# Attention with TensorE's products in source order, two heads' scores together, and low parts of weights by an adding DMA

## The chip, the core and the metric

The kernel runs on one core of one Trainium2 chip. The metric is the device time of one execution in microseconds (us). The engines of the core work beside each other, each in its own order: TensorE (PE in the rows; PEld is its weight load) multiplies into eight banks of PSUM, VectorE (DVE), ScalarE (ACT) and GpSimd (POOL) work on SBUF and PSUM, and SyncE (SP) issues the loads. An instruction waits, by semaphores, until what it reads is there and what it overwrites has been read.

## The reference, cut to what matters

Two layers on a sequence of 512 tokens with 1024 channels, batch 1, all in float32. Layer 0 mixes tokens by differential attention, layer 1 by retention; each layer goes on with a squared-ReLU MLP (1024 to 4096 and back) and a gated embedding. The change bears on the attention above all:

```python
qkv = xn @ w_qkv                                 # 8 heads; q and k: two halves of 64 each, v: 128
q = rms_norm(q, g_q) * (A_DHEAD ** -0.5)
k = rms_norm(k, g_k)
...
s = jnp.einsum('bqhcd,bkhcd->bhcqk', qb, k)      # c: the two halves
s = s + bias[None, :, None]                      # -slope of the head x distance
s = jnp.where(dist[None, None, None] >= 0, s, -jnp.inf)
a = jax.nn.softmax(s, axis=-1)
attn = a[:, :, 0] - lam * a[:, :, 1]
return jnp.einsum('bhqk,bkhe->bqhe', attn, v)
...
o = rms_norm(o, g_sub) * (1.0 - lambda_init)     # per head
return o.reshape(B, S, A_HEADS * A_VDIM) @ w_o
```

## The kernel before, in words

**Numbers in two parts.** Every matrix product is made of three: each float32 operand is split into a high part (`h`, rounded to float32r) and a low part (`l`, the rest), and `mm3` (L177) multiplies high by high, low by high and high by low into the same bank. In the rows the three have lines L179, L180 and L181.

**Weights.** `Weights.load` (L64) brings a block of 128x1024 float32 (512 KB) into one of three `raw` slots, ScalarE casts it to `wh` (L75), and `wl = raw - wh` is made by VectorE (L79). There are five slots each for wh and wl, so block i+5 can only be cast when the last product that reads block i is done. In the attention (blocks 8 to 35) the low part is shared: GpSimd makes one half of 512 columns, VectorE the other (L314).

**Attention.** Channels lie on partitions. The 8 heads go in four groups g of two. For each group and each tile tt of 128 tokens, `pqk` (24 products over the 1024 channels) gives q and k of the group's two heads; `norm_qk` (L346) takes their RMS over ScalarE and VectorE, `scale_qk` (L366) applies it, and `turn_qk` (L375) turns the tile by four transposes into the bank `ptqk`, from which ScalarE and VectorE write qh, ql, kh, kl. `scores(h, i)` (L395) makes the scores of head h for the i-th tile of queries: n = 128(i+1) columns of keys, two halves c of 64 rows, each with three products (kh by qh, kl by qh, kh by ql) into a bank `ps` of its own; the products of the two halves alternate in the source, since they use different rows of TensorE. VectorE evicts each half with the bias (L416), ScalarE exponentiates (L420), VectorE combines the two into `e`. `turn_a` (L433) turns e into `pt` and splits it into aT; `values` (L440) multiplies by v into the bank `po`; `sub_norm` (L453) sums the squares of po by two products into `pn`, ScalarE takes Ln, Exp and Square, VectorE L462 and L464 follow (L464 reads po), and `oT` goes into the output projection (`po__`, L501 on).

**Banks.** PSUM has three banks "mm" (pqk, pv, the projection), two "s" (scores), two "tr" (ptqk, pt, pn) and one "av" (po). A bank is taken again when its readers are done.

**What sets the order.** A plan (L469 to L547) gives each step a position in units of one three-product unit, and the steps are called in the order of these positions. The constants L_TURN, L_S, L_T, L_AV, L_N say how many units behind its inputs a step is called. This is the order of the source; a scheduler then orders each engine's instructions by its own estimate, and may move any product ahead of another. Only SP's loads are kept in program order.

**Layer 1.** Retention ends with eight up products `pu` (L794) whose banks ScalarE copies out (L797). The MLP (L556) begins with two tiles interleaved by `tiles` (L193); the column sums for its norm, `rsm1p`, are called at unit `late_at` of the second of them.

Of the kernel before, what the change touches and what calls it, by code (L numbers as in the profile page):

```python
# [12 lines left out]
AF = mybir.ActivationFunctionType  # L13
# [3 lines left out]
P = 128  # L17
T = 512
# [24 lines left out]
L_TURN = 6  # L43
L_S = 11
# [4 lines left out]
L_S2 = 0.5  # L49
# [3 lines left out]
class Weights:  # L53
# [3 lines left out]
    def __init__(self, tc, pool, order, ahead):  # L57
        self.tc, self.nc, self.pool, self.order, self.ahead = tc, tc.nc, pool, order, ahead
        self.made = []
        self.at = 0  # L60
        self.lo_engines = (self.nc.vector,)
        self.parts = 1

    def load(self):  # L64
# [5 lines left out]
        lo = self.pool.tile([P, 1024], F32R, name=f"wl{i}", tag="wl", bufs=W_BUFS)  # L70
        n = 1024 // self.parts
# [21 lines left out]
def decoder_trunk(ctx: ExitStack, tc, xT, pT, small, dist, decay, ident,  # L93
# [13 lines left out]
    def ps_s(name):  # L107
        return psum("s", 2, name)
# [67 lines left out]

    def mm3(ps, a, b, start, stop):  # L177

        nc.tensor.matmul(ps, a[0], b[0], start=start, stop=False)  # L179
        nc.tensor.matmul(ps, a[0], b[1], start=False, stop=False)  # L180
        nc.tensor.matmul(ps, a[1], b[0], start=False, stop=stop)  # L181
# [53 lines left out]
    def column_sums(ps, pair):  # L235

        nc.tensor.matmul(ps, ones_r, pair[0], start=True, stop=False)
        nc.tensor.matmul(ps, ones_r, pair[1], start=False, stop=True)
# [55 lines left out]
    with tc.tile_pool(name="at", bufs=1) as ap:  # L294
# [19 lines left out]
        W.lo_engines = (nc.gpsimd, nc.vector)  # L314
# [60 lines left out]
        def turn_qk(g, tt):  # L375
# [9 lines left out]
            for j in range(4):  # L385
                nc.tensor.transpose(pt[:, j * P : j * P + P], tf[:, j * P : j * P + P], idn)
# [8 lines left out]
        def scores(h, i):  # L395
            g, j = h // 2, h % 2
            q = (res[g, "q", "h"][:, j, :], res[g, "q", "l"][:, j, :])
            k = (res[g, "k", "h"][:, j, :], res[g, "k", "l"][:, j, :])
# [9 lines left out]
            pss = [ps_s(f"ps{h}{i}{c}") for c in range(2)]  # L408
            for m in range(3):
                for c in range(2):  # L410
                    rows = slice(DH * c, DH * c + DH)
                    a = q[1 if m == 2 else 0][rows, i * P : i * P + P]
                    b = k[1 if m == 1 else 0][rows, 0:n]
                    nc.tensor.matmul(pss[c][:, 0:n], a, b, start=m == 0, stop=m == 2)
            for c in range(2):
                nc.vector.tensor_tensor_reduce(  # L416
                    out=es[c], in0=pss[c][:, 0:n], in1=bias[h][:, T - n : T], op0=ALU.add, op1=ALU.min,
                    scale=1.0, scalar=3e38, accum_out=mn[h][:, i, c : c + 1],
                )
                nc.scalar.activation(  # L420
                    out=es[c], in_=es[c], func=AF.Exp, scale=-1.0, bias=mn[h][:, i, c : c + 1],
                    accum_out=su[h][:, i, c : c + 1],
                )
# [9 lines left out]
        def turn_a(h, kt):  # L433
            n = T - kt * P
            pt = ps_tr(f"pt{h}{kt}")
            for i in range(kt, NT):
                nc.tensor.transpose(pt[:, (i - kt) * P : (i - kt + 1) * P], eT[h, i][:, kt * P : kt * P + P], idn)
# [93 lines left out]
        for g in range(4):  # L531
            s = qk_at[g]
            for tt in range(NT):
# [3 lines left out]
                for j in range(2):  # L537
                    place(e + L_S + L_S2 * j, scores, 2 * g + j, tt)
            t0 = s + NT * KD - 1 + L_T[g]
            for j in range(2):  # L540
# [4 lines left out]
                place(tp + L_AV[g] + L_N, sub_norm, 2 * g + j)  # L545
        for _, _, fn, args in sorted(plan, key=lambda s: s[:2]):
            fn(*args)  # L547
        z, acc = zn, st["acc"]
        W.lo_engines = (nc.vector,)
# [6 lines left out]
    def mlp(z, acc, layer):  # L556
# [3 lines left out]
        with tc.tile_pool(name=f"mlp{layer}", bufs=1) as mp:  # L560
            for c in range(4):
# [14 lines left out]
                tiles(8, begin, unit, end, late if c == 0 else None)  # L576
# [67 lines left out]
    with tc.tile_pool(name="zp", bufs=1) as zp:  # L644
# [12 lines left out]
        with tc.tile_pool(name="ret", bufs=1) as ap:  # L657
# [135 lines left out]
            for m in range(KD):  # L793
                pu = ps_tr(f"pu1{m}")  # L794
# [7 lines left out]
        z, acc = mlp(z, acc, 1)  # L802
# [84 lines left out]
```

## Time and profile before

| | us |
|---|---|
| runs (three) | 1500.09, 1500.62, 1501.07; median 1500.62 |
| profiled execution | 1498.45 |
| its span, first to last instruction | 1496.6 |
| TensorE busy | 1470.9 (98%) |
| VectorE, ScalarE, GpSimd busy | 827.7, 618.7, 183.6 |
| chain that ended last: TensorE's share | 88% |
| attention in the trace | about 29 to 262 |

The chain is followed back from the last instruction, at each step to what released it. TensorE holds most of it, so a microsecond counts if TensorE stands or works longer than it need. Matmuls overlap in the pipeline, so the cost of a product is read as the step from its start to the next start, not as its own duration. "Idle before" in square brackets is time in which the engine had nothing to do before the instruction, with the instruction that released it.

### The profile page before, as it was taken

To read this page: it belongs to the slowest core of one execution; us is meant where nothing else is said; L and a number is where in the kernel's file an instruction comes from. 1 tells how busy PE (TensorE), PEld (TensorE's weight loads), DVE (VectorE), ACT (ScalarE), POOL (GpSimd) and SP (SyncE) were. 2 spreads that over 40 slices of the span, in tenths; PEclk is the share of its full clock that TensorE was granted. 3 is DMA by queue.
4 is the path that set the end of the run, shared out by engine and by line. 5 is a ranking of instruction groups with operands and counts; after the bars stand their busy time and mean duration, and the time that the engine had idled before them with its cause. 6 is when DMAs were issued, how large, how long until landed. Compare 5 with 4: busy or idle time off the path is not lost.

```text
span 1496.6 us, 17071 instructions
## 1 busy us (share of the span) xinstructions
PE 1470.9 (98%) x6668; PEld 1199.6 (80%) x6668; DVE 827.7 (55%) x1217; ACT 618.7 (41%) x966; POOL 183.6 (12%) x128
## 2 busy tenths in 40 slices
PE   9999999899999999999999999999999999999998
PEld 7667667688888888888888888888778888888887
DVE  7887888853434444475464564544584343434455
ACT  6666766541323224344442432433453241323332
POOL 4123223300000000311020110301220000000020
PEclk9999999999999999999999999999999999999999
DMA  6211131243333233232314233132233333333312
GB/s 234 61 57 57 57 113 57 81 116 99 98 92 95 96 99 99 85 99 93 105 51 132 64 99 106 57 127 71 71 99 99 98 94 93 96 98 99 99 57 85
DMA packets 40256, 137.90 MB, mean 92 GB/s; under 512 B 4464, under 2 KB 4976, under 8 KB 40176
## 3 DMA queue, kind: packets, MB, share of 16 engines
q1 hardware_dynamic: 40176, 136.82, 29.5%
q8 instruction: 52, 0.85, 0.2%
q14 instruction: 28, 0.23, 0.0%
HBM read 134.70 MB, written 2.10 MB: 91 GB/s over the span
## 4 chain that ended last, share of the span: by engine, by line
PE 88%; DVE 7%; ACT 2%; issue 1%; POOL 0%; DMA 0%; SPq 0%; POOLq 0%; DVEq 0%; ACTq 0%
PE py L179 8%; PE py L180 8%; PE py L181 8%; PE ph L180 8%; PE ph L181 8%; PE ph L179 8%; PE pg L181 2%; PE pg L180 2%; PE pg L179 2%; PE rv L180 2%; PE rqk L181 2%; PE rqk L180 2%; PE rv L181 2%; PE rv L179 2%; PE rqk L179 2%; PE rg L179 2%
## 5 line engine op out<-in xcount | busy, mean ns | idle before, releaser
L75 ACT CAST wh<-raw 128x1024 fp32r<-128x1024 f32 (+1 forms) x245 | 256.4, 1048 | 620.9 <-PE py L180 235.7
L79 DVE TENSOR_TENSOR wl<-raw,wh 128x1024 fp32r<-128x1024 f32 (+1 forms) x245 | 300.6, 1228 | 60.5 <-ACT wh L75 59.4
L180 PE MATMUL ph<-zl,wh 128*128 128x512 f32 x512 | 200.1, 391 | 3.5 <-DVE zl L160 3.4
L181 PE MATMUL ph<-zh,wl 128*128 128x512 f32 x512 | 199.8, 391 | 0.0
L179 PE MATMUL ph<-zh,wh 128*128 128x512 f32 x512 | 199.5, 390 | 0.1
L179 PE MATMUL py<-hh,wh 128*128 128x512 f32 x512 | 199.2, 389 | 0.0
L180 PE MATMUL py<-hl,wh 128*128 128x512 f32 x512 | 199.2, 389 | 0.0
L181 PE MATMUL py<-hh,wl 128*128 128x512 f32 x512 | 199.2, 389 | 0.0
L582 DVE TENSOR_TENSOR x<-x,py 128x512 f32<-128x512 f32 x64 | 44.0, 688 | 200.0 <-PE py L181 200.0
L572 DVE SCALAR_TENSOR_TENSOR ht<-ph,rsm 128x512 f32<-128x512 f32 x64 | 44.0, 691 | 158.8 <-PE ph L181 158.8
L180 PEld LDWEIGHTS ph<-zl,wh 128*128 128x128 f32 x512 | 96.5, 189 | 25.1 <-DVE zl L160 5.2
L179 PEld LDWEIGHTS ph<-zh,wh 128*128 128x128 f32 x512 | 96.4, 188 | 20.7 <-issue 0.5
L181 PEld LDWEIGHTS ph<-zh,wl 128*128 128x128 f32 x512 | 96.5, 189 | 20.1
L181 PEld LDWEIGHTS py<-hh,wl 128*128 128x128 f32 x512 | 96.1, 188 | 20.1
L179 PEld LDWEIGHTS py<-hh,wh 128*128 128x128 f32 x512 | 96.1, 188 | 20.0
L180 PEld LDWEIGHTS py<-hl,wh 128*128 128x128 f32 x512 | 96.1, 188 | 19.8
L229 POOL TENSOR_TENSOR acc_p<-acc_p,sq 128x512 f32<-128x512 f32 x14 | 24.2, 1727 | 673.7 <-ACT sq L228 673.7
L79 POOL TENSOR_TENSOR wl<-raw,wh 128x512 fp32r<-128x512 f32 x28 | 46.0, 1642 | 90.0 <-ACT wh L75 70.6
L179 PE MATMUL pqk<-wh,zh 128*128 128x512 f32 x128 | 53.6, 419 | 0.0
L179 PE MATMUL pg<-zh,wh 128*128 128x512 f32 (+1 forms) x136 | 51.2, 377 | 0.0
L181 PE MATMUL pg<-zh,wl 128*128 128x512 f32 (+1 forms) x136 | 51.2, 377 | 0.0
L180 PE MATMUL pg<-zl,wh 128*128 128x512 f32 (+1 forms) x136 | 51.2, 376 | 0.0
(874 smaller groups left out, 2762.9 us busy)
## 6 DMA issues: line engine op xcount, KB each, us to landing
raw<-in_w SPq DMA_DIRECT2D x128, 512.0 KB, 3.6
raw<-in_w_qk SPq DMA_DIRECT2D x16, 512.0 KB, 3.7
raw<-in_w_g SPq DMA_DIRECT2D x16, 512.0 KB, 3.6
raw<-in_w_rv SPq DMA_DIRECT2D x16, 512.0 KB, 3.7
raw<-in_w_rqk SPq DMA_DIRECT2D x16, 512.0 KB, 4.4
raw<-in_w_rg SPq DMA_DIRECT2D x16, 512.0 KB, 3.6
raw<-in_w_ro SPq DMA_DIRECT2D x16, 512.0 KB, 3.6
raw<-in_w_o SPq DMA_DIRECT2D x8, 512.0 KB, 3.6
```

Of the source, the lines that this page charges most:

```text
L75: nc.scalar.copy(out=hi[:, s], in_=raw[:, s])
L79: e.tensor_tensor(out=lo[:, r], in0=raw[:, r], in1=hi[:, r].bitcast(F32), op=ALU.subtract)
L179: nc.tensor.matmul(ps, a[0], b[0], start=start, stop=False)
L180: nc.tensor.matmul(ps, a[0], b[1], start=False, stop=False)
L181: nc.tensor.matmul(ps, a[1], b[0], start=False, stop=stop)
L229: nc.gpsimd.tensor_tensor(out=acc, in0=acc, in1=sq, op=ALU.add)
L572: nc.vector.scalar_tensor_tensor(out=t, in0=s[1], scalar=0.0, in1=rs, op0=ALU.max, op1=ALU.mult)
L582: nc.vector.tensor_tensor(out=x[m], in0=x[m], in1=ps, op=ALU.add)
```

## The change

Four edits. The products and transposes that the attention's plan calls are kept in the order of the source on TensorE (`pe`, `fixed`). `scores(g, i)` makes both heads of a group at once: for i = 0 and 1 (up to 256 columns) the heads share the two banks, each in its half of the columns, and their twelve products stand together; for i = 2 and 3 each head has its own two banks and its six products, one head after the other. L_TURN goes from 6 to 8 and L_S from 11 to 13 units. The low parts of blocks 8 to 35 are made by ScalarE, which writes -raw rounded into wl, and a DMA issued by GpSimd that adds raw to it; VectorE and GpSimd make no half of them any more. In layer 1 the up products alternate between the banks "tr" and "s", and the MLP's column sums are called at unit 5 in place of 2.

```diff
@@ -40,13 +40,12 @@
 RAW_BUFS, W_BUFS, SLOTS = 3, 5, 30
 
 L_SCALE = 4
-L_TURN = 6
-L_S = 11
+L_TURN = 8
+L_S = 13
...
-L_S2 = 0.5
...
@@ -68,6 +68,14 @@
         raw = self.pool.tile([P, 1024], F32, name=f"raw{i}", tag="raw", bufs=RAW_BUFS)
         hi = self.pool.tile([P, 1024], F32R, name=f"wh{i}", tag="wh", bufs=W_BUFS)
         lo = self.pool.tile([P, 1024], F32R, name=f"wl{i}", tag="wl", bufs=W_BUFS)
+        if self.by_dma:
+
+            self.tc.keep_in_program_order(nc.sync.dma_start(out=raw, in_=src))
+            nc.scalar.copy(out=hi, in_=raw)
+            nc.scalar.activation(out=lo, in_=raw, func=AF.Copy, scale=-1.0)
+            nc.gpsimd.dma_start(out=lo, in_=raw, accum_op=ALU.add)
+            self.made.append((hi, lo))
+            return
...
+    fixed = {"on": False}
+
+    def pe(ins):
+
+        if fixed["on"]:
+            tc.keep_in_program_order(ins)
+
     def mm3(ps, a, b, start, stop):
 
-        nc.tensor.matmul(ps, a[0], b[0], start=start, stop=False)
-        nc.tensor.matmul(ps, a[0], b[1], start=False, stop=False)
-        nc.tensor.matmul(ps, a[1], b[0], start=False, stop=stop)
+        pe(nc.tensor.matmul(ps, a[0], b[0], start=start, stop=False))
+        pe(nc.tensor.matmul(ps, a[0], b[1], start=False, stop=False))
+        pe(nc.tensor.matmul(ps, a[1], b[0], start=False, stop=stop))
...
@@ -311,7 +326,7 @@
             for tt in range(NT):
                 mm3(pv[tt], token(z[k], tt), block(w, k), k == 0, k == KD - 1)
         rst_columns(acc, rst, "prst0")
-        W.lo_engines = (nc.gpsimd, nc.vector)
+        W.by_dma = True
...
             tf = qkt.pop((g, tt))[0]
             pt = ps_tr(f"ptqk{g}{tt}")
             for j in range(4):
-                nc.tensor.transpose(pt[:, j * P : j * P + P], tf[:, j * P : j * P + P], idn)
+                pe(nc.tensor.transpose(pt[:, j * P : j * P + P], tf[:, j * P : j * P + P], idn))
...
-        def scores(h, i):
-            g, j = h // 2, h % 2
-            q = (res[g, "q", "h"][:, j, :], res[g, "q", "l"][:, j, :])
-            k = (res[g, "k", "h"][:, j, :], res[g, "k", "l"][:, j, :])
+        def scores(g, i):
+
+            n = P * (i + 1)
+            joint = n <= T // 2
+            pss = [ps_s(f"ps{g}{i}{c}") for c in range(2)] if joint else None
+            made = []
+            for j in range(2):
+                h = 2 * g + j
+                q = (res[g, "q", "h"][:, j, :], res[g, "q", "l"][:, j, :])
+                k = (res[g, "k", "h"][:, j, :], res[g, "k", "l"][:, j, :])
+                s = [pss[c][:, j * (T // 2) : j * (T // 2) + n] if joint else ps_s(f"ps{h}{i}{c}")[:, 0:n] for c in range(2)]
+                for m in range(3):
+                    for c in range(2):
+                        rows = slice(DH * c, DH * c + DH)
+                        a = q[1 if m == 2 else 0][rows, i * P : i * P + P]
+                        b = k[1 if m == 1 else 0][rows, 0:n]
+                        pe(nc.tensor.matmul(s[c], a, b, start=m == 0, stop=m == 2))
+                if joint:
+                    made.append((h, s))
+                else:
+                    weigh(h, i, s)
+            for h, s in made:
+                weigh(h, i, s)
+
+        def weigh(h, i, pss):
             if i == 0:
                 bias[h] = ap.tile([P, T], F32, name="bias", tag="bias", bufs=2)
                 nc.gpsimd.tensor_scalar(
@@ -405,16 +441,9 @@
                 su[h] = ap.tile([P, NT, 2], F32, name="su", tag="su", bufs=3)
...
-            pss = [ps_s(f"ps{h}{i}{c}") for c in range(2)]
-            for m in range(3):
-                for c in range(2):
-                    rows = slice(DH * c, DH * c + DH)
-                    a = q[1 if m == 2 else 0][rows, i * P : i * P + P]
-                    b = k[1 if m == 1 else 0][rows, 0:n]
-                    nc.tensor.matmul(pss[c][:, 0:n], a, b, start=m == 0, stop=m == 2)
             for c in range(2):
                 nc.vector.tensor_tensor_reduce(
-                    out=es[c], in0=pss[c][:, 0:n], in1=bias[h][:, T - n : T], op0=ALU.add, op1=ALU.min,
+                    out=es[c], in0=pss[c], in1=bias[h][:, T - n : T], op0=ALU.add, op1=ALU.min,
...
@@ -534,8 +563,7 @@
                 e = s + (7, 15, 30, 34)[tt]
                 place(e + L_SCALE, scale_qk, g, tt)
                 place(e + L_TURN, turn_qk, g, tt)
-                for j in range(2):
-                    place(e + L_S + L_S2 * j, scores, 2 * g + j, tt)
+                place(e + L_S, scores, g, tt)
...
@@ -543,17 +571,19 @@
                     place(tp, turn_a, 2 * g + j, kt)
                     place(tp + L_AV[g], values, 2 * g + j, kt)
                 place(tp + L_AV[g] + L_N, sub_norm, 2 * g + j)
+        fixed["on"] = True
         for _, _, fn, args in sorted(plan, key=lambda s: s[:2]):
             fn(*args)
+        fixed["on"] = False
         z, acc = zn, st["acc"]
-        W.lo_engines = (nc.vector,)
+        W.by_dma = False
...
-    def mlp(z, acc, layer):
+    def mlp(z, acc, layer, late_at=2):
...
-                tiles(8, begin, unit, end, late if c == 0 else None)
+                tiles(8, begin, unit, end, late if c == 0 else None, late_at)
...
             for m in range(KD):
-                pu = ps_tr(f"pu1{m}")
+                pu = (ps_tr if m % 2 == 0 else ps_s)(f"pu1{m}")
                 up_unit(pu, wu, p1, m)
                 t = zslot(f"pus{m}", F32)
                 nc.scalar.copy(out=t, in_=pu)
...
-        z, acc = mlp(z, acc, 1)
+        z, acc = mlp(z, acc, 1, late_at=5)
         gated_embedding(z, acc, None, 1, True, made=made)
```

Column sums and `turn_a` are wrapped in `pe` in the same way. Three places show what the order of the instructions becomes. In the names, the digits of `ps` are head (for i = 0 and 1 group), tile i and half c; those of `ptqk` and `pqk` are group and tile; those of `po`, `pn` are the head; `po05__` is the output projection.

TensorE, scores of the last tile (i = 3) of heads 0 and 1, before:

```order
L414 MATMUL ps030_800<-kh0_454,qh0_452 128x512
L414 MATMUL ps031_801<-kh0_454,qh0_452 128x512
L414 MATMUL ps030_800<-kl0_455,qh0_452 128x512
L414 MATMUL ps031_801<-kl0_455,qh0_452 128x512
L414 MATMUL ps030_800<-kh0_454,ql0_453 128x512
L414 MATMUL ps031_801<-kh0_454,ql0_453 128x512
L386 MATMUL ptqk10_819<-idn_314,qkt_721 128x128 x4
L179 MATMUL pqk11_735<-wh11_385,zh0_6_157 128x512
L414 MATMUL ps130_830<-kh0_454,qh0_452 128x512
L414 MATMUL ps130_830<-kl0_455,qh0_452 128x512
L414 MATMUL ps130_830<-kh0_454,ql0_453 128x512
L180 MATMUL pqk11_735<-wl11_386,zh0_6_157 128x512
```

and after:

```order
L426 MATMUL ps030_816<-kh0_476,qh0_474 128x512
L426 MATMUL ps031_817<-kh0_476,qh0_474 128x512
L426 MATMUL ps030_816<-kl0_477,qh0_474 128x512
L426 MATMUL ps031_817<-kl0_477,qh0_474 128x512
L426 MATMUL ps030_816<-kh0_476,ql0_475 128x512
L426 MATMUL ps031_817<-kh0_476,ql0_475 128x512
L426 MATMUL ps130_833<-kh0_476,qh0_474 128x512
L426 MATMUL ps131_834<-kh0_476,qh0_474 128x512
L426 MATMUL ps130_833<-kl0_477,qh0_474 128x512
L426 MATMUL ps131_834<-kl0_477,qh0_474 128x512
L426 MATMUL ps130_833<-kh0_476,ql0_475 128x512
L426 MATMUL ps131_834<-kh0_476,ql0_475 128x512
```

Before, head 1's halves stand apart, with products of pqk between; now all twelve stand in a row.

TensorE, the column sums of head 5 and the values of head 6, before:

```order
L237 MATMUL pn5_2549<-osq5h_2503,ones_r_67 128x512
L238 MATMUL pn5_2549<-osq5l_2504,ones_r_67 128x512
L180 MATMUL po06__2581<-oT0l_1177,wh27_1853 128x512
L181 MATMUL po06__2581<-oT0h_1176,wl27_1854 128x512
L179 MATMUL po06__2581<-oT1h_1384,wh27_1853 128x512
L180 MATMUL po06__2581<-oT1l_1385,wh27_1853 128x512
L181 MATMUL po06__2581<-oT1h_1384,wl27_1854 128x512
L179 MATMUL po06__2581<-oT2h_1557,wh27_1853 128x512
L180 MATMUL po06__2581<-oT2l_1558,wh27_1853 128x512
L181 MATMUL po06__2581<-oT2h_1557,wl27_1854 128x512
L179 MATMUL po06__2581<-oT3h_1731,wh27_1853 128x512
L180 MATMUL po06__2581<-oT3l_1732,wh27_1853 128x512
```

and after:

```order
L252 MATMUL pn5_2533<-osq5h_2487,ones_r_67 128x512
L253 MATMUL pn5_2533<-osq5l_2488,ones_r_67 128x512
L194 MATMUL po6_2548<-aT0h_2496,v101h_1153 128x512
L195 MATMUL po6_2548<-aT0l_2497,v101h_1153 128x512
L196 MATMUL po6_2548<-aT0h_2496,v101l_1154 128x512
L194 MATMUL po05__2506<-oT3h_1712,wh26_1834 128x512
```

Before, the values po6 come eight rows behind the last one shown; now they stand directly behind pn5.

ScalarE, around the cast of block 13 and the keys of group 1's first tile, before:

```order
L420 ACTIVATE e3_798,su_501<-e3_798,mn_500 128x512
L420 ACTIVATE es_799,su_501<-es_799,mn_500 128x512
L159 ACTIVATE kh1_817<-ptqk10_819,sm_61 128x2x128
L420 ACTIVATE e3_828,su_522<-e3_828,mn_521 128x512
L349 ACTIVATE qks_851<-pqk11_735,rst_182 128x512
L420 ACTIVATE es_829,su_522<-es_829,mn_521 128x512
L351 ACTIVATE qkt_853<-pqk11_735,rst_182 128x512
L356 ACTIVATE qky_858<-qkr_855 128x8
L357 ACTIVATE qky_858<-qky_858 128x8
L75 CAST wh13_663<-raw13_662 128x1024
```

and after:

```order
L75 ACTIVATE wl13_660<-raw13_658 128x1024
L74 CAST wh13_659<-raw13_658 128x1024
L167 ACTIVATE kh1_852<-ptqk10_854,sm_61 128x2x128
L449 ACTIVATE e0_899,su_898<-e0_899,mn_897 128x128
L449 ACTIVATE es_900,su_898<-es_900,mn_897 128x128
L449 ACTIVATE e0_912,su_911<-e0_912,mn_910 128x128
```

Before, kh1 stands seven rows ahead of the cast wh13; now wl13 and wh13 stand ahead of kh1. On TensorE the products behind which these wait and those that wait for kh1 are, after:

```order
L194 MATMUL pqk13_870<-wh8_364,zh0_1_100 128x512
L195 MATMUL pqk13_870<-wl8_365,zh0_1_100 128x512
L196 MATMUL pqk13_870<-wh8_364,zl0_1_101 128x512
L194 MATMUL pqk12_863<-wh9_371,zh0_2_109 128x512
L195 MATMUL pqk12_863<-wl9_372,zh0_2_109 128x512
L196 MATMUL pqk12_863<-wh9_371,zl0_2_110 128x512
L426 MATMUL ps100_881<-kh1_852,qh1_850 128x128
L426 MATMUL ps101_882<-kh1_852,qh1_850 128x128
L426 MATMUL ps100_881<-kl1_853,qh1_850 128x128
```

Block 13 takes the slot of block 8, whose last product is that with zl0_1; three products of pqk12 stand between it and the scores that read kh1.

## Rows read from the trace of the kernel before

**Rows 1.** Busy time by stage: stretch, length, then busy us (xcount) per engine, clock, DMA.
```profile
29.00:262.00 233.00, 223.27 (x1082) 165.67 (x1082) 190.18 (x507) 152.07 (x348) 66.55 (x52) 1.00 0.23 73
...
300.00:1060.00 760.00, 759.91 (x3440) 633.52 (x3439) 376.12 (x424) 278.18 (x364) 64.00 (x41) 1.00 0.30 93
```

**Rows 2.** TensorE's waits from 29 to 300 us: us in total, times, longest.
```profile
PE ph L180 <- DVE zl L160: 3.4, 1, 3.4
PE ptqk L386 <- DVE qkt L370: 1.9, 2, 1.5
PE pn L237 <- DVE aT0l L157: 1.7, 1, 1.7
PE pn L237 <- DVE kl L160: 1.5, 1, 1.5
PE ptqk L386 <- DVE qku L359: 1.5, 2, 0.9
```

**Rows 3.** TensorE in order of time (start us, us, operation): first visit, a pair, last visit.
```profile
42.91 0.39 PE L181 MATMUL pqk<-wh,zl 128*128 128x512 f32 x1
43.14 0.39 PE L179 MATMUL pqk<-wh,zh 128*128 128x512 f32 x1
43.46 0.33 PE L414 MATMUL ps<-kh,qh 64*128 64x128 f32 x2
...
71.57 0.50 PE L414 MATMUL ps<-kh,qh 64*128 64x512 f32 x2
...
72.14 0.40 PE L414 MATMUL ps<-kh,ql 64*128 64x512 f32 x2
...
229.67 0.49 PE L414 MATMUL ps<-kh,qh 64*128 64x512 f32 x1 [0.32 <-DVE mn L416]
...
230.56 0.51 PE L179 MATMUL po__2488<-oT1h,wh 128*128 128x512 f32 x1
230.90 0.40 PE L180 MATMUL po__2488<-oT1l,wh 128*128 128x512 f32 x1
```

**Rows 4.** VectorE's low parts of weights (busy, mean ns); then 59.69 to 61.58 us.
```profile
L79 DVE TENSOR_TENSOR wl<-raw,wh 128x512 fp32r<-128x512 f32 x26 | 24.2, 930 | 7.5 <-ACT wh L75 7.3
...
59.69 1.79 POOL L79 TENSOR_TENSOR wl<-raw,wh 128x512 fp32r<-128x512 f32 x1 [3.53 <-ACT wh L75]
...
60.25 1.33 DVE L359 TENSOR_TENSOR qku<-qky 128x8 f32<-128x8 f32 x2
```

**Rows 5.** TensorE in order of time, layer 1: the two waits there.
```profile
1065.31 0.50 PE L179 MATMUL pu<-p10h,wh 128*128 128x512 f32 x1 [1.49 <-ACT pus L797]
...
1104.57 0.50 PE L237 MATMUL rsm1p<-rsm1sh,ones_r 128*128 128x512 f32 x1 [1.89 <-ACT rsm1sh L156]
```

**Rows 6.** VectorE's evictions of scores: one in order of time, then a group.
```profile
72.57 0.69 DVE L416 CUSTOM_DVE_ANT_0 e<-ps,bias 128x512 f32<-128x512 f32 x1 [0.27 <-PE ps L414]
...
L416 DVE CUSTOM_DVE_ANT_0 es<-ps,bias 128x384 f32<-128x384 f32 x8 | 4.4, 554 | 1.0 <-PE ps L414 0.9
```

**Rows 7.** Order of time from pn to the freed bank, head 4.
```profile
213.49 0.39 PE L238 MATMUL pn<-osq4l,ones_r 128*128 128x512 f32 x1
...
215.97 0.69 DVE L462 SCALAR_TENSOR_TENSOR osu<-pn,osu 128x512 f32<-128x512 f32 x1 [1.46 <-ACT osu L461]
...
216.58 0.74 DVE L464 SCALAR_TENSOR_TENSOR osq<-po,gs,osq 128x512 f32<-128x512 f32 x1
```

**Rows 8.** A weight cast behind its release, in order of time; then a group of ScalarE.
```profile
121.83 0.40 PE L181 MATMUL pv<-wh,zl 128*128 128x512 f32 x1
...
122.26 1.05 ACT L75 CAST wh<-raw 128x1024 fp32r<-128x1024 f32 x1 [1.55 <-PE pv L181]
...
L159 ACT ACTIVATE kh<-ptqk,sm 128x256 fp32r<-128x256 f32 x16 | 7.5, 471 | 7.7 <-DVE ql L160 7.6
```

**Rows 9.** DMA issues of before: operation, count, KB each, median us to landing.
```profile
raw<-in_w SPq DMA_DIRECT2D x128, 512.0 KB, 3.6
...
dst<-in_dist SPq DMA_DIRECT2D x1, 256.0 KB, 5.5
```

More of the change, by code (lines that the diff above doesn't have):

```diff
@@ L62, in __init__ @@
         self.parts = 1
+        self.by_dma = False
     def load(self):
@@ L235, in column_sums @@
     def column_sums(ps, pair):
-        nc.tensor.matmul(ps, ones_r, pair[0], start=True, stop=False)
-        nc.tensor.matmul(ps, ones_r, pair[1], start=False, stop=True)
+        pe(nc.tensor.matmul(ps, ones_r, pair[0], start=True, stop=False))
+        pe(nc.tensor.matmul(ps, ones_r, pair[1], start=False, stop=True))
     def rs_rows(acc, name):
@@ L436, in turn_a @@
             for i in range(kt, NT):
-                nc.tensor.transpose(pt[:, (i - kt) * P : (i - kt + 1) * P], eT[h, i][:, kt * P : kt * P + P], idn)
+                pe(nc.tensor.transpose(pt[:, (i - kt) * P : (i - kt + 1) * P], eT[h, i][:, kt * P : kt * P + P], idn))
             aT[h, kt] = hilo(ap, f"aT{kt}", pt[:, 0:n], shape=(P, n), bufs=1 if kt < 2 else 2)
```

## The prediction, as put on record before the changed kernel ran

> **What bounds the kernel now.** I read the table by stage first, then the waits of TensorE, then TensorE's own order of time. Between 300 and 1060 us TensorE is busy without a break, so nothing can be gained there but by fewer products. In the attention (29 to 262 us) it is busy 223.27 of 233 us, VectorE 190.18 and ScalarE 152.07, at a granted clock of 1.00, the upper of the two levels (2.4 GHz) [rows 1]. So the attention loses time in two ways: the 10 us in which TensorE stands, and products that take longer than they need. The list of waits gives the first: in the attention the longest are behind VectorE (ptqk 1.9 and 1.5, pn 1.7 and 1.5), and after it one of 3.4 us stands where the MLP begins [rows 2]. The order of time gives the second. A full product (512 columns) follows the one before it in 0.23 us (42.91 to 43.14) [rows 3]. Where TensorE goes from full products to scores (64 rows) the step is 0.32 us (43.14 to 43.46), and the step after the scores is 0.34 us (230.56 to 230.90) [rows 3]: 0.10 and 0.11 us too much per visit. The two halves of a score tile start together when they stand side by side (the "x2" at 71.57) [rows 3], and six products then take as long (0.90 us for 512 columns) as three of one half alone (229.67 to 230.56, 0.89 us) [rows 3].
>
> **What the change takes away.** (a) Visits to the scores. TensorE goes there 46 times before (first and last in rows 3) and 16 times after, four tiles in each of four groups: 30 x 0.21 = 6.3 us. Ten second tiles were torn into two lone halves before: five of 512 columns, four of 384 and one of 256. Each paid a whole set of three products twice: 0.89, and by columns some 0.67 and 0.45 us; 4.45 + 2.68 + 0.45 = 7.6 us. Together 13.9 us.
> (b) VectorE loses its half of 28 low parts, 0.930 us each in the mean [rows 4], 26 us in all, and GpSimd its half. The latter also stretches VectorE: two operations on 128x8 took 1.33 us while GpSimd worked on wl for 1.79 us [rows 4]. So the four long waits behind VectorE in the attention should go: 1.9 + 1.7 + 1.5 + 1.5 = 6.6 us. The smaller ones I leave. At the end of the attention VectorE loses two halves, while ScalarE gets two casts more, ahead of the wait of 3.4 us: I take 1.0 (0 to 2).
> (c) The second layer: the up products use four banks in place of two, which ends the wait of 1.49 us for ScalarE's copy; the column sums stand nine products (2.0 us) later, which hides their wait of 1.89 us [rows 5]. What ends last there next is the reciprocal behind the sums, and it ends when it did. Together 3.4 us.
>
> **What it adds.** (d) The second head. For 384 and 512 columns its six products stand directly behind the first head's six, as the order shows, and there are two banks. A bank comes free when VectorE has evicted it: at 512 columns 72.57 + 0.69 - 72.14 = 1.12 us after the last product's start [rows 3, 6]. The next product would have started 0.23 after it, so the first half waits 0.9, and the second half one more eviction, of which I take 0.65 (they overlap a little at their ends): 1.55 us. For 384 columns an eviction takes 0.554 in place of 0.69 [rows 6]; I take 1.3. Eight places, 4 x (1.55 + 1.3) = 11.4 us. Before, the scheduler put other products there. If VectorE is in another operation, it is more, by half of one.
> (e) The chain behind the column sums pn of a head. From the second product of pn (213.49) three passes of ScalarE and L462 and L464 of VectorE lead to the end of L464 at 216.58 + 0.74 = 217.32, 3.83 us later [rows 7]. Until then the only "av" bank is taken. In the pinned order po6 stands directly behind pn5 (wait 3.6), po3 1.1 us behind pn2 (2.7), po2 some 2.5 us behind pn1 (1.3), and po1 0.2: 7.8 us. The bank of pn itself is free when L462 has ended, 215.97 + 0.69 - 213.49 = 3.17; pt51, pn0 and ptqk13 find it taken: 1.8 + 0.4 + 0.5 = 2.7 us. Sum 10.5 us. Before, the values of the next head stood further behind.
> (f) Casts ahead of the keys. The scheduler now puts wl and wh of a block back to back on ScalarE. Both need the slot of the block five before, so they start only when its last product has ended: 122.26, behind a product that starts at 121.83 [rows 8]. Three times the kh of the next score tile stands behind them (kh1, kh2, kh3). Worked from that last product's start: 0.43 to the cast, 2 x 1.05 for the casts, 0.47 for kh [rows 8], as much again for kl on VectorE (an estimate from kh's size), 0.04 between: 3.5 us. TensorE has four products (0.91 us) and an entry before the pair of products that needs kl: about 1.2. So 2.35 us each for two places and 1.83 for the third, where four transposes stand between: 6.5 us.
> (g) Elsewhere ScalarE has 28 x 1.05 = 29 us more to do, in 81 us of idle time. At four places (ptqk02, ptqk22, the scores of tile 1, po2) one or two casts stand ahead of a chain that TensorE waits for. Bounds 0 and 4 x 2.1 = 8.4; I take a little over one cast each, 4.8 us, because in the order most of them find a cast already under way.
> (h) The adding DMA. No DMA of the trace adds and none is issued by GpSimd, so its length is bounded by other transfers: 3.6 us for 512 KB in the median, 5.5 for the slowest landing [rows 9], of 256 KB. It runs behind wl's cast, beside wh's. In the tight blocks the first product that reads wl stands 7.7 us of products behind the release of the slot; chain 0.43 + 1.05 + 3.6 = 5.1, with the upper bound 7.0. So I cost it at nothing; the products of the block before hide it, and past 7.7 every microsecond is TensorE's. On SP's queue the next load of raw must now wait for the add, and behind it stand later loads, x among them; they are three blocks ahead, and I cost that at nothing. On GpSimd the bias, osq's low part and osu now stand between issues of a DMA in place of 1.6 us of work, which can only help them.
>
> One rule speaks against (h). Row first: while GpSimd used SBUF, small work of VectorE took several times as long [rows 4]. The Trainium skill ("SBUF — State Buffer", sections "SBUF: two separate sides" and "Who interferes with whom") calls the port pair of these two engines an exclusive lock, and adds that a DMA issued by GpSimd has its descriptors written by GpSimd, so that a VectorE operation in a two-port mode holds the DMA up. The first half agrees with the row; the second no run here shows yet. By it the adds would be late, as in the second rival below.
>
> **The sum**, against the profiled execution's own 1498.45 us: 1498.45 - 13.9 - 6.6 - 1.0 - 3.4 + 11.4 + 10.5 + 6.5 + 4.8 = 1506.75. That execution lies 2.17 us under the median of the runs shown, so **1508.9 us**. With the bounds of (b) and (g) and half an operation of VectorE in (d) its own range is 1503 to 1515.
>
> **The rivals.** First, the casts do not stand in the way: the place in the order tells nothing of time, and where TensorE already waits for a bank, ScalarE catches up, so that (f) and (g) hide behind (d) and (e). For it speaks that ScalarE keeps 50 us of idle time, against it that (f) counts from a product just ahead. 1508.9 - 11.3 = 1497.6.
> Second, the adds land late: a landing of 7.8 us, 2.3 over the slowest shown, would hold each of the six tight blocks (9, 10, 11, 21, 22, 23) by about 1.6 us: 1508.9 + 9.6 = 1518.5. It decides from 6.2 us on. For it speaks only the rule above and that VectorE is still busy most of the time, against it the 3.6 us of all loads.
> Third, the other way: with VectorE free of 26 us and of GpSimd's grip, the remaining waits behind it go too, and half of (e) is worked off where TensorE stood already: 1497.6 - 5.3 = 1492.3.
> Fourth, the pinning buys nothing and costs nothing, and the layer's gain alone is left, 1500.6 - 3.4 = 1497.2: I count it with the first.
>
> **How the numbers follow.** Forecast 0.43, first rival 0.27, second 0.17, third 0.13. Within 0.2% (about what a measurement of this kernel can tell from no change) is 1497.6 to 1503.6. The forecast lies above it but for 0.05 of its chance; the first rival lies on its lower edge: 0.13 faster, 0.12 same, 0.02 slower. So faster 0.13 + 0.13 = 0.26, same 0.05 + 0.12 = 0.17, slower 0.38 + 0.02 + 0.17 = 0.57. The range leaves out the top of the second rival and the bottom of the third, 1492 to 1520.
>
> **What would show it.** (a) holds if the step after the scores stays 0.34 us and comes 16 times. (d) holds if the second head's products wait some 0.9 and 0.65 us behind VectorE's evictions at eight places; (e) if po6 waits about 3.6 us behind VectorE's product of po5 with gs, and po3 2.7; (f) if kh1, kh2 and kh3 start directly after a wh cast and TensorE waits for kl; (h) if adds land in under 5.5 us and no product that reads wl waits for a DMA; (c) if pu and rsm1p leave the list of waits. I am wrong if TensorE's waits in the attention sum to well under 30 us, or if the products' steps do not shorten.

## The result, and the profile after

The changed kernel takes 1511.3 us in the median of its runs (1510.09 to 1513.97), the kernel before 1500.36 beside it: ratio 1.0077, 95% interval 1.0065 to 1.0090. It is slower by some 11 us; 1508.9 had been forecast. The profiled execution is the longest of its runs, 1513.97 us, 15.5 above the profiled one of before. Its granted clock over the whole run is 0.991 in the mean; that of the other three is 0.993, and that of the profiled run of before 0.999.

Where the 15.5 us arose is read from the start of the same products in both traces. First the products that open and close the stretch, before (columns: start us, us, operation):

```profile
29.46 0.49 PE L179 MATMUL pqk<-wh,zh 128*128 128x512 f32 x1
...
260.56 0.39 PE L179 MATMUL po__2796<-oT6h,wh 128*128 128x512 f32 x1
```

and after:
```profile
29.68 0.49 PE L194 MATMUL pqk<-wh,zh 128*128 128x512 f32 x1
...
283.57 0.39 PE L194 MATMUL po__2780<-oT6h,wh 128*128 128x512 f32 x1
```

The stretch from the first product of q and k to the first one that reads oT6 holds the same products in both and takes 231.1 us before and 253.89 after: 22.8 us more. From there to the MLP's steady part the changed kernel makes up 3.5 us, and in layer 1 another 4.0: there is no wait before pu any more and 0.23 us in place of 1.89 + 0.23 at the column sums. In total 22.8 - 3.5 - 4.0 = 15.3; the other 0.2 stands ahead of the first product (29.46 and 29.68).

Within the attention, two views. The table by stage of the changed kernel (columns as in [rows 1]):

```profile
29.00:262.00 233.00, 200.84 (x982) 153.33 (x981) 152.73 (x459) 159.91 (x352) 39.48 (x44) 0.95 0.50 120
```

VectorE is busy 152.73 us in place of 190.18, GpSimd 39.48 in place of 66.55, ScalarE 159.91 in place of 152.07: the low parts have left two engines, as meant (the same 233 us hold less of the attention after, so ScalarE does not show all of its 29 us more). But TensorE is busy 200.84 us in place of 223.27 in the same 233 us, and its granted clock is 0.95 in place of 1.00 [rows 1]. The list of waits says behind what it stands (29 to 285 us; total, times, longest):

```profile
PE po L194 <- DVE osq L493: 10.9, 4, 4.3
PE ps L426 <- DVE mn L445: 9.7, 13, 1.2
PE ps L426 <- ACT kh L167: 4.4, 3, 1.8
PE pt L466 <- DVE osu L491: 1.9, 1, 1.9
PE ptqk L401 <- DVE qku L374: 1.6, 2, 0.9
PE pn L253 <- POOL osq4l L165: 1.0, 1, 1.0
PE ptqk L401 <- DVE aT1l L165: 0.5, 1, 0.5
PE ps L426 <- DVE kl L168: 0.4, 2, 0.2
```

With four more ahead of pn, behind what it reads and behind aT0l (2.3 us), they sum to 32.7 us. The list of before sums to 9.1 in its attention, of which [rows 2] show the four longest. Where the clock falls, the order of time and a table by short stretches show, here around the wait ahead of po3 (the 4.3 us above):

```profile
148.40 0.39 PE L253 MATMUL pn<-osq2l,ones_r 128*128 128x512 f32 x1
...
149.32 0.38 PE L466 MATMUL pt<-idn,e 128*128 128x128 f32 x2
149.52 0.69 ACT L487 ACTIVATE osq<-pn,eps 128x512 f32<-128x512 f32 x1
...
153.95 0.79 PE L194 MATMUL po<-aT0h,v001h 128*128 128x512 f32 x1 [4.26 <-DVE osq L493]
```

```profile
149.00:152.00 3.00, 0.70 (x5) 0.33 (x3) 2.08 (x9) 2.83 (x8) 0.00 (x0) 1.00 0.51 175
...
153.00:156.00 3.00, 2.05 (x5) 1.66 (x6) 2.21 (x5) 0.99 (x2) 0.62 (x1) 0.50 0.00 0
156.00:159.00 3.00, 3.00 (x9) 2.32 (x8) 0.47 (x2) 0.00 (x0) 0.00 (x0) 0.50 0.00 0
...
160.00:162.00 2.00, 2.00 (x11) 1.68 (x10) 0.77 (x2) 0.48 (x1) 0.00 (x0) 1.00 0.00 0
```

TensorE starts its last transposes at 149.32 and stands until 153.95, for VectorE's L493 that reads the old po. At some 152.7, in that wait, the granted clock goes from the upper level (2.4 GHz) to the lower (1.2 GHz, 0.50 in the rows), and it is at the lower until after 159; products there start 0.43 us apart in place of 0.23. Such falls stand at six places of the attention, from 74 to 259 us. One more, from 303 us, stands where the MLP begins, and the trace of before has its like there. 0.05 of 233 us is 11.7 us; about 0.6 of it lies in the wait itself (half of 152.7 to 153.95), so the clock costs some 11 us. That is for the profiled execution; by their clock over the whole run (0.993 for 0.991) it cost the other three some 3 us less, an estimate of 0.002 of 1510. Waits and clock together are 32.7 - 9.1 + 11 = 34.6, so the visits and pairs must have given back 34.6 - 22.8 = 11.8, a remainder and not a measurement of its own.

### The profile page after: what moved, and what is told of

It is laid out like the page before. It is cut to its first block, busy times and chain, and to the rows that moved or that the text cites. A ratio compares the mean times of both kernels' runs of the same rounds, so it can differ in the third digit from the quotient of the medians.

```text
span 1512.2 us, 17055 instructions
## 1 busy us (share of the span) xinstructions
PE 1469.0 (97%) x6668; PEld 1205.2 (80%) x6668; DVE 800.6 (53%) x1189; ACT 642.5 (42%) x994; POOL 163.3 (11%) x128
## 4 chain that ended last, share of the span: by engine, by line
PE 89%; ACT 5%; DVE 4%; issue 1%; DMA 1%; POOL 0%; SPq 0%; DVEq 0%; ACTq 0%; POOLq 0%
PE py L196 8%; PE py L195 8%; PE py L194 8%; PE ph L195 7%; PE ph L196 7%; PE ph L194 7%; PE rg L194 2%; PE rg L195 2%; PE pg L194 2%; PE pg L196 2%; PE pg L195 2%; PE rv L194 2%; PE rqk L196 2%; PE rv L196 2%; PE rqk L194 2%; PE rg L196 2%
## 5 line engine op out<-in xcount | busy, mean ns | idle before, releaser
L83 ACT CAST wh<-raw 128x1024 fp32r<-128x1024 f32 (+1 forms) x217 | 227.2, 1049 | 609.8 <-PE py L195 235.7
L87 DVE TENSOR_TENSOR wl<-raw,wh 128x1024 fp32r<-128x1024 f32 (+1 forms) x217 | 275.0, 1268 | 48.8 <-ACT wh L83 47.7
L195 PE MATMUL ph<-zl,wh 128*128 128x512 f32 x512 | 200.2, 391 | 2.8 <-DVE zl L168 2.8
L195 PE MATMUL py<-hl,wh 128*128 128x512 f32 x512 | 199.2, 389 | 0.0
L195 PEld LDWEIGHTS ph<-zl,wh 128*128 128x128 f32 x512 | 96.6, 189 | 24.7 <-DVE zl L168 4.7
L195 PEld LDWEIGHTS py<-hl,wh 128*128 128x128 f32 x512 | 96.1, 188 | 20.0
L195 PE MATMUL pqk<-wl,zh 128*128 128x512 f32 x128 | 52.0, 406 | 0.0
L196 PE MATMUL pqk<-wh,zl 128*128 128x512 f32 x128 | 51.9, 405 | 0.0
```

The lines of the kernel that those rows point to most:

```text
L83: nc.scalar.copy(out=hi[:, s], in_=raw[:, s])
L87: e.tensor_tensor(out=lo[:, r], in0=raw[:, r], in1=hi[:, r].bitcast(F32), op=ALU.subtract)
L195: pe(nc.tensor.matmul(ps, a[0], b[1], start=False, stop=False))
L196: pe(nc.tensor.matmul(ps, a[1], b[0], start=False, stop=stop))
```

## The experiments

Two theories stood against each other. One: the loss comes from the order that is fixed on TensorE, by waits that the forecast listed one by one, and by the clock that falls behind them. The other: it comes from the adding DMA with its second cast on ScalarE. All times below are medians, and each ratio is to the kernel before on the same chip; a ratio is taken over the runs and differs a little from the quotient of the two medians.

**Layer 1 alone** (before, with the two edits of layer 1):

```diff
-                pu = ps_tr(f"pu1{m}")
+                pu = (ps_tr if m % 2 == 0 else ps_s)(f"pu1{m}")
...
-        z, acc = mlp(z, acc, 1)
+        z, acc = mlp(z, acc, 1, late_at=5)
```

> The kernel before with the two edits of layer 1 alone (up products over four banks, column sums at unit 5). Both theories expect the same here, it sizes the term: the two waits of 1.49 and 1.89 us and the slower first products behind them go, so 3.4 to 4.1 us less than the kernel before, about 1496.5 us. If the sums come so late that the reciprocal ends later, less than 2.5 us.

1495.0 us against 1498.64, ratio 0.9968 (0.9955 to 0.9981): 3.6 us, as sized.

**The adding DMA alone** (before, with the new branch of `load`):

```diff
-        W.lo_engines = (nc.gpsimd, nc.vector)
+        W.by_dma = True
```

> The kernel before with the low parts of blocks 8 to 35 by the adding DMA alone: the scheduler still orders TensorE, the scores stand as before. Theory of the pinned order (the loss comes from waits that the order of the products fixes): no loss, VectorE's waits of 6.6 us shrink and a few behind ScalarE's casts come, 1493 to 1502 us. Rival (the adding DMA and the double casts are what costs): slower than before by 5 us or more, 1505 to 1512 us, with waits behind kh, exps or the DMA.

1494.43 us against 1498.64, ratio 0.9970 (0.9959 to 0.9982): 4.2 us faster. TensorE's waits in the attention shrink to this and one more of 0.2 us (29 to 262 us; 0.8 us at the projection, which before has too, behind 262 us, is left out):

```profile
PE pn L246 <- POOL osq1l L165: 0.6, 1, 0.6
PE ps L422 <- DVE mn L424: 0.6, 1, 0.6
PE ptqk L394 <- DVE qkt L378: 0.5, 1, 0.5
PE pqk L188 <- DMA wl<-raw: 0.3, 1, 0.3
PE pn L245 <- DVE kl L168: 0.3, 1, 0.3
```

Nothing is left of the four waits of [rows 2] in the attention but pieces of 0.5 and 0.3 us, and the blocks' low parts hold TensorE for 0.3 us in all, by the DMA. The list sums to 2.5 us in place of 9.1, so the 6.6 us of (b) went. The second theory falls with this run: left to the scheduler, the adding DMA is a gain.

**The changed kernel, not pinned:**

```diff
-        fixed["on"] = True
```

> The changed kernel with one line out: the products are not pinned, the scheduler orders TensorE; joint scores, adding DMA and layer 1 stay. Pinned order at fault: the waits of second heads (9.8 us), of the av bank (10.9) and the falls of the clock go for the most part, 1488 to 1500 us. Rival (adding DMA at fault): stays above 1505 us.

1485.39 us, ratio 0.9904 (0.9889 to 0.9919). One line makes 26 us (1511.3 to 1485.39), and turns a loss of 11 into a gain of 13. By stage:

```profile
29.00:262.00 233.00, 226.90 (x1120) 171.89 (x1121) 169.72 (x491) 178.79 (x384) 46.16 (x53) 1.00 0.57 137
```

The clock is back at 1.00 and TensorE busy 226.90 us of 233. This is also the kernel that beats both.

**Pinned, but with the old low parts:**

```diff
-        W.by_dma = True
+        W.lo_engines = (nc.gpsimd, nc.vector)
```

> The changed kernel with the low parts of the attention made by GpSimd and VectorE as before, everything else as changed. Pinned order at fault: the waits of second heads and of the av bank stay (about 20 us), those behind casts lose one cast each (3 x 1.05), VectorE has 26 us more and its waits grow: 1508 to 1518 us. Rival (adding DMA at fault): back to about the kernel before less layer 1, 1497 to 1502 us.

1525.39 us, ratio 1.0172 (1.0157 to 1.0187), worse than either theory gave. The waits of the second heads and of the av bank, which the order makes, are there as before, and others behind VectorE come on top (29 to 300 us):

```profile
PE po L194 <- DVE osq L493: 9.8, 4, 4.2
PE ps L426 <- DVE mn L445: 9.4, 11, 1.4
PE ptqk L401 <- DVE qkt L385: 5.6, 4, 2.5
PE ps L426 <- DVE kl L168: 2.5, 2, 2.0
```

In the changed kernel ptqk waited 1.6 us in all, behind qku, and kl made 0.4. The relief that the adding DMA brings is worth 14 us in the fixed order and 4 where the scheduler orders; that TensorE cannot step around a late VectorE in a fixed order would explain it, and these waits fit.

**The old plan pinned, and nothing else** (before, with `pe` around the attention's products):

```diff
+        fixed["on"] = True
         for _, _, fn, args in sorted(plan, key=lambda s: s[:2]):
             fn(*args)
+        fixed["on"] = False
```

> The kernel before with its products pinned to the source order and nothing else (old plan, scores one head after the other, old low parts). If the pinning is what costs, whatever the scores: 1515 us or more. Rival (the twelve products in a row are what costs, and a pinned order with separate heads is harmless): 1497 to 1504 us.

1547.97 us, ratio 1.0309 (1.0293 to 1.0324). Pinning alone costs 47 us, with separate heads and the old low parts. So the joint heads do not make the loss. The run before this one has them and the later positions on the same pin and the same low parts, and stands at 1.0172, some 20 us less, of which layer 1 is 3.6: together they make a pinned order less bad.

**Values of heads 2 and 3 later:**

```diff
-L_T = (23, 21, 21, 19)
-L_HEAD = (16, 14, 16, 3)
+L_T = (23, 24, 21, 19)
+L_HEAD = (16, 18, 16, 3)
```

> The changed kernel with the steps of heads 2 and 3 later (L_T of group 1 from 21 to 24, L_HEAD of group 1 from 14 to 18), so that po2 and po3 stand some 3.8 us of products behind pn1 and pn2. If the av bank's waits and the clock's falls behind them are what costs there: the waits of 2.4 and 4.3 us go and with them the double fall of the clock at 153 us (3.4 us), 1500 to 1503 us. Rival (the chain only moves: something else is late at the same place): 1508 us or more.

1508.6 us, ratio 1.0049 (1.0029 to 1.0069): 2.7 us less than the changed kernel, where 8 to 11 were expected, and its interval overlaps that of the changed kernel (1.0065 to 1.0090). Its runs spread from 1505.75 to 1514.11, and the profiled one is the longest, so the trace is of a longer run than the median. The waits of po2 and po3 did go there. In their place (TensorE's waits; then TensorE and ScalarE in order of time):

```profile
PE ptqk L401 <- DVE qku L377: 6.0, 1, 6.0
PE po L194 <- DVE osq L493: 4.2, 2, 3.5
```

```profile
179.75 1.08 PE L401 MATMUL ptqk<-idn,qkt 128*128 128x128 f32 x4 [6.03 <-DVE qku L377]
...
174.56 0.62 ACT L164 CAST oT3h<-osq 128x512 fp32r<-128x512 f32 x1 [2.21 <-DVE osq L494]
175.09 0.68 ACT L364 ACTIVATE qks<-pqk,rst 128x512 f32<-128x512 f32 x1
175.67 0.68 ACT L366 ACTIVATE qkt<-pqk,rst 128x512 f32<-128x512 f32 x1
```

The values stand later, and so does their chain on the in-order engines. ScalarE holds oT3h, which waits 2.21 us for VectorE's L494, and behind it stand qks and qkt of the next tile; ptqk22 waits 6.0 us for the norm that begins there. The rival was nearer: the median lies in its range, and in the trace the wait moved.

**Second heads apart:**

```diff
...
-                place(e + L_S, scores, g, tt)
+                if tt < 2:
+                    place(e + L_S, scores, g, tt)
+                else:
+                    place(e + L_S, scores, g, tt, (0,))
+                    place(e + L_S + 2.5, scores, g, tt, (1,))
```

> The changed kernel with the second head's scores of tiles 2 and 3 placed 2.5 units behind the first head's, still pinned. The second heads' waits (9.8 us) go, eight visits come back (1.7 us). If the clock's falls follow the waits, the falls at 74, 122 and 194 us go too (5.1 us): 1496 to 1500 us. Rival (the falls have another cause): 1502 to 1505 us with as many falls as the changed kernel.

1500.51 us, ratio 1.0000 (0.9991 to 1.0009): 10.8 us less than the changed kernel, half a microsecond above the range that the first theory gave (1496 to 1500) and below the rival's. TensorE's waits for evictions of scores:

```profile
PE po L194 <- DVE osq L493: 9.9, 4, 4.3
PE ps L426 <- DVE mn L445: 1.9, 3, 1.0
```

1.9 us in place of 9.7, and the wait at po is what it was. The falls of the clock at 74, 122 and 194 us, each behind such waits, are gone, but others stand elsewhere: the mean over the attention is 0.96.

**Zero products where TensorE stood** (`zero_r` is a matrix of zeros, so the products add nothing to the bank that they go into):

```diff
...
+            if kt == 0 and h in (3, 6):
+                ps, b = (cur[1], z[0][0]) if h == 3 else (st["ps"][5], oT[0][0])
+                for _ in range(18 if h == 3 else 15):
+                    pe(nc.tensor.matmul(ps, zero_r, b, start=False, stop=False))
             if kt == 0:
                 po[h] = ps_s(f"po{h}") if h == AH - 1 else ps_av(f"po{h}")
```

> The changed kernel with products by a matrix of zeros where TensorE stood: 18 ahead of po3 (4.1 us) and 15 ahead of po6 (3.4 us), added into a bank that is being summed, so that they add nothing. The time until po3 and po6 is the same. If the clock falls because TensorE stood, the falls at 153 and 259 us go: 5.1 us less, 1505 to 1507 us. Rival (the falls do not follow from standing): 1510 to 1513 us.

1508.59 us, ratio 1.0047 (1.0029 to 1.0065), 2.7 us less than the changed kernel in the median; its runs spread from 1504.86 to 1510.67. The profiled executions differ by 5.2 us (1508.79 and 1513.97). The place ahead of po3 once more (the view opens in the middle of the zero products and shows 16 of the 18), and by stretches:

```profile
148.19 3.89 PE L475 MATMUL pqk<-zh,zero_r 128*128 128x512 f32 x16
152.13 0.50 PE L194 MATMUL po<-aT0h,v001h 128*128 128x512 f32 x1
```

```profile
151.00:154.00 3.00, 2.95 (x13) 2.11 (x12) 2.33 (x5) 0.98 (x2) 0.62 (x1) 1.00 0.00 0
154.00:157.00 3.00, 3.00 (x16) 2.51 (x15) 1.39 (x3) 0.74 (x2) 0.00 (x0) 1.00 0.00 0
```

po3 starts no earlier relative to its chain, but the clock stays at 1.00 through the stretch that was at 0.50 in the changed kernel, and it does so behind po6 too. That TensorE stood is thus what made the clock fall there. The gain in the median is half of the 5.1 us expected, and the two intervals just meet, so its size is not settled. Elsewhere in the attention the falls of the changed kernel at 122 and 194 us have their like, those at 74 and 85 us have not, although the waits ahead of them are the same, and one has come behind the wait at po2. The clock over the whole run is 0.994 to 0.998 in the four runs, so how much falls differs from run to run, and what decides that is open.

**The adding DMA and layer 1 together, old plan, not pinned:** the edits of the first two runs.

> The kernel before with the adding DMA and the layer 1 edits, without joint scores, old plan, not pinned. If the gains add up: 4.2 and 3.6 us less than before, 1490 to 1493 us, and what the unpinned kernel has beyond that (5 to 6 us) belongs to the joint scores and the plan's constants. Rival (the joint scores bring nothing, the gains feed each other): 1485 to 1488 us.

1488.49 us, ratio 0.9921 (0.9907 to 0.9936). It lies between the two ranges that were given. By the medians it is 11.7 us, where 3.6 + 4.2 add up to 7.8; by the ratios 0.79% for 0.62%, which the intervals allow. In one place the trace shows what the one gives the other: with the adding DMA alone, the clock had fallen to 0.59 in the stretch from 1099 to 1103 (1.6 us), behind the wait at layer 1's column sums, and the edit of layer 1 removes that wait. The unpinned kernel's ratio of 0.9904 is 2.5 us better, but the intervals overlap: what the joint scores bring by themselves is small and not settled.

**The unpinned kernel with two details turned back**, a run for each: L_TURN and L_S at 6 and 11; and the second heads of tiles 2 and 3 as a step half a unit later.

> The unpinned kernel with L_TURN and L_S back at 6 and 11. If the scheduler's order makes the plan's positions secondary: 1483 to 1488 us, as the unpinned kernel. Rival (the later positions carry the gain): 1489 us or more.

> The unpinned kernel with the second head's scores of tiles 2 and 3 as a step of their own, half a unit later, as in the kernel before. Unpinned, TensorE waits only 0.2 us for evictions of scores, so nothing is left to gain: 1484 to 1488 us. Rival (two heads in one step still cost): below 1483 us.

1486.32 us (0.9906, 0.9890 to 0.9923) and 1486.19 us (0.9907, 0.9892 to 0.9922). Neither detail can be told from the unpinned kernel: where the scheduler orders, these positions matter less than the intervals can tell.

**The cast twice** (the changed kernel; the pass that writes wl is doubled, so that ScalarE has 29 us more):

```diff
             nc.scalar.activation(out=lo, in_=raw, func=AF.Copy, scale=-1.0)
+            nc.scalar.activation(out=lo, in_=raw, func=AF.Copy, scale=-1.0)
```

> The changed kernel with the pass that writes wl on ScalarE made twice for each of the 28 blocks, so that three casts of 1.05 us stand where two stood. If casts ahead of kh and of the head chains are on TensorE's path: 1.05 us more at ps100, ps210 and ps300 each and some at ptqk02, ptqk22, po2 and po3, with a fall of the clock or two, 1515 to 1521 us. Rival (the casts hide behind other waits): 1510 to 1513 us.

1536.24 us, ratio 1.0243 (1.0225 to 1.0260): 25 us more than the changed kernel, where 4 to 10 were expected. That casts stand on TensorE's path is right, the size is not:

```profile
PE ps L427 <- ACT kh L168: 13.8, 4, 6.2
```

```profile
29.00:262.00 233.00, 194.53 (x908) 148.10 (x907) 138.80 (x430) 168.09 (x350) 35.80 (x41) 0.90 0.46 111
```

The wait for kh is 13.8 us in place of 4.4, and one of 6.2 us at ps210: three passes, the head chain and qh all stand ahead of it. The clock is 0.90 over the attention, another 0.05 of 233 us. An engine with idle time in the mean may have none to give at a fixed place.

## Why the prediction was right, and where it was not

The forecast, its sign and its range hold: 1508.9 forecast, 1511.3 measured. The mechanism holds too: the fixed order makes the waits that were listed, nearly place by place, and the runs above show that the change loses by the pinning. But that the medians lie only 2.4 us apart is in part luck. A term is missing, other errors took some 4 of its 11 us back, and in the profiled execution, against which the sum was made, 7.2 us are left (1506.75 and 1513.97); the profiled execution of before lies 2.2 us under its median and that of after 2.7 above its own, and without that 2.4 are left.

**The missing term is the clock.** The sum had every wait and no cost of standing beyond the time stood. The granted clock of the attention, 1.00 before [rows 1], became 0.95: some 11 us. The trace of before held the warning: behind the wait of 3.4 us of [rows 2] the granted clock is 0.58 from 284 to 287 us and 0.85 to 290, and the sum has nothing for it. The row of the first stretch (columns as in [rows 1]):

```profile
284.00:287.00 3.00, 3.00 (x9) 2.35 (x9) 2.26 (x4) 0.00 (x0) 0.00 (x0) 0.58 0.52 142
```

**The waits were right in kind and nearly in sum.** Forecast for the attention were 11.4 + 10.5 + 6.5 + 4.8 us added and 6.6 of 9.1 removed, so 35.7 in all; measured 32.7, above the 30 under which the prediction called itself wrong.
- (d) second heads: 9.7 in place of 11.4, behind VectorE's evictions, as said. In order of time, for heads 0 and 1:

```profile
65.45 0.34 PE L426 MATMUL ps<-kh,ql 64*128 64x384 f32 x2
66.66 0.44 PE L426 MATMUL ps<-kh,qh 64*128 64x384 f32 x1 [0.87 <-DVE mn L445]
67.69 0.44 PE L426 MATMUL ps<-kh,qh 64*128 64x384 f32 x1 [0.59 <-DVE mn L445]
```

The two halves wait 0.87 and 0.59 us, where 1.3 together had been taken.
- (e) the chain of a head: 10.9 us at four po and 1.9 at pt51 in place of 10.5; po6 waited 3.48 where 3.6 had been worked out. po3 was under-sized, 4.26 for 2.7: the rows above show Ln (L487) starting at 149.52, 1.12 us behind pn's last product, because qks and qkt of the next tile stand ahead of it on ScalarE; before it was 0.43.
- (f) casts ahead of the keys: 4.4 us behind kh and 0.4 behind kl in place of 6.5, at the three places named. ps100, all three engines:

```profile
79.44 0.39 PE L195 MATMUL pqk<-wl,zh 128*128 128x512 f32 x1
...
79.67 0.39 PE L196 MATMUL pqk<-wh,zl 128*128 128x512 f32 x1
...
79.87 1.06 ACT L75 ACTIVATE wl<-raw 128x1024 fp32r<-128x1024 f32 x1 [1.05 <-PE pqk L195]
...
80.83 1.03 ACT L74 CAST wh<-raw 128x1024 fp32r<-128x1024 f32 x1
...
81.77 0.47 ACT L167 ACTIVATE kh<-ptqk,sm 128x256 fp32r<-128x256 f32 x1
82.27 0.48 DVE L168 SCALAR_TENSOR_TENSOR kl<-ptqk,sm,kh 128x256 fp32r<-128x256 f32 x1 [1.34 <-ACT kh L167]
...
82.28 0.33 PE L426 MATMUL ps<-kh,qh 64*128 64x128 f32 x2 [1.55 <-ACT kh L167]
...
82.81 0.33 PE L426 MATMUL ps<-kl,qh 64*128 64x128 f32 x2 [0.20 <-DVE kl L168]
```

The order is the one written down: wl, wh, kh, kl, with TensorE standing 1.55 + 0.20 us. From the block's last product (79.67) to the end of kl (82.27 + 0.48) it is 3.08 us in place of 3.5: wl's cast starts 0.20 behind that product and not 0.43, since the slot of wl is free one product earlier, when L195 has read it, and the two casts take 1.90 in place of 2.10.
- (g) four places, 4.8 us: two of them came, 1.6 us at ptqk02 and ptqk22. po2 waited 2.4 in place of 1.3.

**The gains.** (a) 13.9 forecast, 11.8 by difference; its sign came, 16 visits in the trace and a step of 0.33 or 0.34 us behind 12 of them, the rest being at a lower clock or ahead of transposes or a little longer; (b) of the four waits behind VectorE 0.3 us behind aT0l is left, and what stands behind qku is counted under (g); the tail gave 3.5 in place of 1.0, the largest miss among the gains; (c) 4.0 in place of 3.4. So the clock, 11 us too few, was covered in part by waits 3.0 too many, the tail 2.5, layer 1 0.6, while (a) was 2.1 too many.

**(h) the adding DMA** held TensorE once, a weight load by 0.4 us. From issue to landing it took 4.5 to 8.3 us, 5.1 in the median, more than the 3.6 taken and, at its longest, more than the 5.5 of [rows 9] and the 7.8 of the second rival; the products of the block before hid it nonetheless: that one entry is all that the lists of waits have for the 28. The Trainium skill ("DMA: Bandwidth & Descriptors", section "Anatomy of one DMA — SWDGE (gpsimd) path") gives 2.0 us and the bytes divided by 436,000 a microsecond, an estimate of 3.2 us for 512 KB; the trace shows 5.1 for this adding one, and the measurement decides. By the Trainium skill ("SBUF — State Buffer", section "Who interferes with whom") VectorE in a two-port mode can hold up the writing of descriptors for such a DMA; no run here separates that. With VectorE busy 152.73 of 233 us the adds came early enough all the same.

Of the rivals, the first (casts hidden) fell: the waits stand at kh in the trace, and doubling the casts made them 13.8 us. The second (late adds) did not come: at least one landing was longer than its 7.8 us, but TensorE waited 0.4 us in all. The third did not come in the pinned order; its price has half of (e) alone, and the remaining waits behind VectorE that it names, 9.1 - 6.6 = 2.5 us, are not in it. The fourth (pinning costs nothing) fell with the runs that take the pin away or set it alone, 26 and 47 us. What no run settled: how often the clock falls in a run, and how much the joint scores are worth alone.

## What to carry to other kernels

Pin an order only if every wait in it has been counted against the length of the chain that ends it; here one line of pinning cost 26 us, while the adding DMA and the edit of layer 1 gained 4.2 and 3.6 alone. When a sum is made of waits, add a term for the clock: look in the trace for the stretches behind the longest waits that are there already. A step that is moved takes its whole chain with it on the engines that run in order, so after moving it read what now stands behind that chain.

## What was not expected of the hardware

The granted clock fell to 0.50 in or behind waits of TensorE, and with zero products in the wait it did not; but not behind every one: around po2, with a wait of 2.4 us, it stayed at 1.00 (columns as above):

```profile
132.00:136.00 4.00, 1.94 (x10) 1.36 (x8) 2.07 (x4) 2.30 (x5) 0.26 (x2) 1.00 0.90 139
136.00:140.00 4.00, 3.68 (x17) 3.14 (x18) 1.65 (x3) 2.83 (x4) 1.24 (x2) 1.00 0.77 254
```

In the run with zero products at po3 and po6 the same wait at po2 (2.38 us) stands as it was, and there the clock is 0.58 and 0.57 from 134 to 138 us. The other way round, the waits of 1.21 + 0.19 and 1.55 us at 73 and 80 us, behind which the changed kernel's clock fell, stand there to the hundredth, and the clock stays at 1.00. So the length of a wait does not tell by itself whether the clock falls.

The cost of a fall is of the same order as the wait ahead of it: 0.50 from 152.7 to about 159.5 is 3.4 us of lost clock (0.6 of it within the wait) for 4.3 us stood, and the other five falls of the attention lost 1.7 us each, behind waits of 1.4 to 3.5 us.
